# One scan for both directions in the S5 token mixer of a two-layer diffusion block

## The chip, the cores and the metric

The kernel runs on one core of a Trainium2 chip, in one launch that computes both layers. The metric is the device time of that launch in microseconds. Three runs of the kernel before gave 2297.36, 2298.63 and 2300.72 us, a median of 2298.63 us.

## The reference, cut to what matters

Two layers work on 256 context tokens and 512 latent tokens of width 1024. Each layer normalises the tokens, projects them and feeds four token mixers in parallel (A attention, B Fourier mixing, C a bidirectional diagonal state space "S5", D retention). Each mixer's output is projected to 1024 columns, gated, and added to a sum; an output projection and an MLP follow. The change is in mixer C alone:

```
lam_bar, b_bar = s5_discretise(...)             # per group of 16 channels: 64 complex states
bu = einsum('blgh,gph->blgp', u, b_bar)         # 16 groups
x[t] = lam_bar * x[t-1] + bu[t]                 # forward: context, then latent, carried over
                                                # backward: the context reversed, then the latent reversed
y = Re(C_f x_f) + Re(C_b x_b) + d * u           # readout and direct term
y = gelu(y);  val, gate = split(y @ w_glu);  out = val * sigmoid(gate)
```

## The kernel before, in words

All matrix products split both factors into a high and a low part (`split`, L289: ScalarE copies the high part at L293, VectorE subtracts at L294) and run three matmuls for each product (L239 through `gemm` and `mm3`). Weights come by DMA on SyncE into `raw` (two buffers) or `raws` (one), and become `whi`/`wlo` (three buffers) or `whis`/`wlos` (two).

The S5 stage (`s5`, from L1502) works in chunks of 8 tokens: 96 chunks hold the 768 tokens. A group pair g (eight of them, two groups of channels each) runs like this. `states(g)` loads the pair's operators (one DMA into `S`, two into `M`), multiplies the chunks by them on TensorE (the result lies in a PSUM tile `b` of which there are two), turns each chunk's sum by a precomputed rotation so that the decay becomes real, scans over the chunks, and turns back. The chunk axis has 128 columns: 96 chunks and a second copy of the 32 context chunks, because the backward direction starts with the context. Forward states lie in rows 0 to 63 and backward states in rows 64 to 127, so two scans run per real and imaginary part, L1568 forward on one half of the rows and L1570 backward on the other. The products of the turns run on VectorE, their sums and differences on GpSimd (`sx<-sx` and `sX<-sx` in the rows). `readout(g)` runs 12 matmuls (two passes for each of 6) into the same PSUM tile, adds the direct term `d * u` on VectorE (`Y`), and applies gelu on ScalarE, GpSimd and VectorE. The direct term is prepared ahead of the loop by four GpSimd multiplies of `sb`.

The loop calls `states(g + 1)` ahead of `readout(g)`, and between them `self.tick(2)`, which takes two steps of a background job: the merge of mixer A (`merge_steps`), whose steps alternate between a gate product (weights of 512 KB, 24 times 512 columns and in layer 0 also 24 times 256) and a branch product (6 times as much), with a VectorE multiply (`gate`) and a GpSimd add (`xy`) behind each branch product. Two of the 16 steps run ahead of the stage. After the loop the second feature transpose, the GLU products and the merge of mixer C follow; the first two gate products of that merge need nothing of the stage.

The order on each engine is set ahead by a planner: it simulates the program with modelled durations and gives each engine the most urgent ready instruction, where earlier in the program is more urgent. On the chip each engine then runs its list in order. A tile whose buffers are all in use holds the instruction that wants one.

The operators are prepared earlier (`s5_prep`): in layer 0 beside the merge of mixer B (about 104 to 205 us), in layer 1 beside the MLP of layer 0. `s5_rot` builds the rotations by doubling, the first 10 groups on VectorE and 6 on GpSimd; `s5_ops` builds the operators and the `strip`, from which `M` is read.

Of the kernel before, what the change touches and what calls it, by code (L numbers as in the profile page):

```python
# [9 lines left out]
F32 = mybir.dt.float32  # L10
# [3 lines left out]
AF = mybir.ActivationFunctionType  # L14
OP = mybir.AluOpType
# [8 lines left out]
NTOK = NCTX + NLAT  # L24
DEPTH = 2
# [184 lines left out]
class Net:  # L210
# [207 lines left out]
    def build(self):  # L418
        tc, nc = self.tc, self.nc
        with ExitStack() as es:  # L420
# [14 lines left out]
            self.xsp = self.dr.tile([KT, 128, NTOK], F32, name="xsp")  # L435
            self.scr = [self.dr.tile([8, 128, 6 * 256], F32, name=f"scr{l}") for l in range(DEPTH)]
            self.par = [self.dr.tile([128, 16 * NPAR + 48], F32, name=f"par{l}") for l in range(DEPTH)]
# [946 lines left out]
    def s5_ops(self, l, sp, bc, pr, pi, wr, wi, Br, Bi, Vr, Vi):  # L1384
        nc = self.nc
# [30 lines left out]
        def second(g, R, Wr, Wi):  # L1416
# [41 lines left out]
    def s5_rot(self, l, sp, rot):  # L1458

        nc = self.nc  # L1460
        F, B = slice(0, 64), slice(64, 128)
        T = lambda n, s, b=1: sp.tile([128] + list(s), F32, name=n, bufs=b)
        er, ei = T("er", [16, 128]), T("ei", [16, 128])
        nc.vector.memset(er[:, :, 0:1], 1.0)
        nc.vector.memset(ei[:, :, 0:1], 0.0)
        gr, gi = T("gr", [16, 1], 2), T("gi", [16, 1], 2)
        nc.vector.tensor_copy(gr[:, :, 0], rot[:, 0])
        self.ts(gi[F, :, 0], rot[F, 1], -1.0)
        nc.vector.tensor_copy(gi[B, :, 0], rot[B, 1])
        n = 1  # L1470
        while n < 128:
            m = min(n, 32)
            for o in range(0, n, m):
                t = [T(f"ce{k}", [16, 32], 1) for k in range(2)]
# [15 lines left out]
            if n > 4:  # L1490
                yield
        for k, e in enumerate((er, ei)):
            nc.vector.memset(e[F, :, 127:128], 0.0)
            nc.vector.memset(e[B, :, 0:1], 0.0)
        for _ in range(4):
            yield
        for k, e in enumerate((er, ei)):
            c = 1024 + 256 * k
            nc.sync.dma_start(self.scr[l][:, :, c:c + 256].rearrange("g p c -> p g c"), e.rearrange("p (g q) n -> p g (q n)", q=2))
        yield  # L1500

    def s5(self, l, sp, segs):  # L1502
# [22 lines left out]
        for g in range(16):  # L1525
# [8 lines left out]
        d4 = dv[:96].rearrange("c (g h) -> c g h", g=16)  # L1534
        for g in range(0, 16, 4):
            self.tt(Uc[:96, g:g + 4], Uc[:96, g:g + 4], d4[:, g:g + 4, None, :].to_broadcast([96, 4, 8, 16]), OP.mult, gp)
        G = T("sd", [8, 256])
        def states(g):

            S = T("S", [6, 2, 128], 2)  # L1540
            r8 = T("r8", [256], 2)
            self.act(r8.rearrange("p (q c) -> p q c", q=2), ex[:, 2 * g:2 * g + 2, None].to_broadcast([128, 2, 128]))
            nc.vector.memset(r8[F, 128:129], 0.0)
            nc.vector.memset(r8[B, 127:128], 0.0)
            nc.sync.dma_start(S, self.scr[l][g])
            M = T("M", [2, 128], 2)
            st = self.strip[l][2 * g:2 * g + 2]
            for q in range(2):
                nc.sync.dma_start(M[:, q], bass.AP(tensor=st.tensor, offset=st.offset + q * 3840,
                                                   ap=[[16, 8], [240, 16], [1, 128]]))  # L1550
            p = self.pb()
            for k in range(2):
                for q in range(2):
                    self.mm(p[:, 512 * k + 128 * q:512 * k + 128 * q + 128], S[:, k, q], U[:, 2 * g + q], True, True)
            w = p.rearrange("p (k c) -> p k c", k=2)[:, :, 0:256]
            f = lambda t: t.rearrange("p k q c -> p k (q c)")
            cs, sc = f(S[:, 4:6]), f(S[:, 5:3:-1])
            n = lambda: T("sx", [2, 256], 4)
            t1, t2, W = n(), n(), n()
            self.tt(t1, w, cs, OP.mult)  # L1560
            self.tt(t2, w, sc, OP.mult)
            self.tt(W[:, 0], t1[:, 0], t1[:, 1], OP.subtract, gp)
            self.tt(W[:, 1], t2[:, 0], t2[:, 1], OP.add, gp)
            Z = n()
            gp.memset(Z[F, :, 0:1], 0.0)
            gp.memset(Z[B, :, 255:256], 0.0)
            for k in range(2):
                nc.vector.tensor_tensor_scan(out=Z[F, k, 1:256], data0=r8[F, 1:256], data1=W[F, k, 0:255], initial=0.0,  # L1568
                                             op0=OP.mult, op1=OP.add)
                nc.vector.tensor_tensor_scan(out=Z[B, k, 254::-1], data0=r8[B, 254::-1], data1=W[B, k, 255:0:-1], initial=0.0,  # L1570
                                             op0=OP.mult, op1=OP.add)
            X = T("sX", [2, 256], 2)
            t1, t2 = n(), n()
            self.tt(t1, Z, cs, OP.mult)
            self.tt(t2, Z, sc, OP.mult)
            self.tt(X[:, 0], t1[:, 0], t1[:, 1], OP.add, gp)
            self.tt(X[:, 1], t2[:, 1], t2[:, 0], OP.subtract, gp)
            if segs[0][0] == 0:
                v = X[B].rearrange("p k (q c) -> p (k q) c", q=2)
                self.act(v[:, :, 0:32], v[:, :, 96:128])  # L1580
            return p, S, M, X

        def readout(g, p, S, M, X):
            for q in range(2):
                o = p[:96, 256 + 128 * q:384 + 128 * q]
                c = slice(128 * q, 128 * q + 96)
                self.mm(o, U[:, 2 * g + q, 0:96], M[:, q], True, False)
                self.mm(o, X[:, 0, c], S[:, 2, q], False, False)
                self.mm(o, X[:, 1, c], S[:, 3, q], False, True)
            Y = sp.tile([96, 2, 8, 16], F32, name="Y", bufs=2)  # L1590
            Z = sp.tile([96, 2, 8, 16], F32, name="Z", bufs=2)
            self.tt(Y, p[:96, 256:512].rearrange("c (q t h) -> c q t h", q=2, t=8), Uc[:96, 2 * g:2 * g + 2, ::-1, :], OP.add)
# [16 lines left out]

        r = states(0)  # L1610
        for g in range(8):
            n = states(g + 1) if g < 7 else None
            self.tick(2)
            readout(g, *r)
            r = n
            if g == 4:
                gT = [feature(0, *(self.fix.tile([128, NTOK], F32R, name="tmp", bufs=2) for _ in range(2)))]
# [5 lines left out]
        for m in range(2):  # L1623
            pv, pg = self.pb(), self.pb()
            self.gemm(pg, self.wk(w, 2, 256 + 128 * m, 384 + 128 * m), gT, segs)
            self.gemm(pv, self.wk(w, 2, 128 * m, 128 * m + 128), gT, segs)
            t = sp.tile([128, NTOK], F32, name="sd")
# [40 lines left out]
```

## Time and profile before

| of the profiled execution | |
|---|---|
| its time | 2295.92 us |
| its span in the trace | 2294.1 us |
| TensorE busy | 2172.5 us, 95% |
| VectorE, ScalarE, GpSimd busy | 1501.1, 727.3 and 329.3 us |
| mean granted TensorE clock | 0.981 |
| median of three runs | 2298.63 us |

The S5 stages lie at 538 to 674 us (layer 0) and 1733 to 1843 us (layer 1). In the rows, PE is TensorE, DVE VectorE, ACT ScalarE, POOL GpSimd and SPq the queue of SyncE. `b<-sa,S` are the chunk sums, `b<-M,sa` and `b<-S,sX` the readout, `b<-ident,sd` the feature transposes, `mm<-...` the background merge. "Idle before" is the time in which the engine had nothing running ahead of the instruction, with the instruction that ended it.

### The profile page before, as it was taken

The numbers are of one execution on the slowest core, as the hardware profiler recorded it, in microseconds if no ns is written. First come the engines' busy times: TensorE is split into PE (matmuls) and PEld (weight loads), VectorE is DVE, ScalarE is ACT, GpSimd is POOL, SyncE is SP. The second block draws the span as 40 slices with busy tenths as digits, with TensorE's granted clock in tenths as the row PEclk, the third lists the DMA queues.
The fourth block names the chain that finished last, engine by engine and source line by source line (L and its number), as shares of the span: only waits on it lengthen the run. The fifth ranks groups of instructions, "written<-read, shape, count | busy, mean of one in ns | idle before, by whom it ended". The sixth has DMA issues, their size and how long they took to land.

```text
span 2294.1 us, 32460 instructions
## 1 busy us (share of the span) xinstructions
PE 2172.5 (95%) x12438; PEld 1848.2 (81%) x12438; DVE 1501.1 (65%) x3283; ACT 727.3 (32%) x1226; POOL 329.3 (14%) x373
## 2 busy tenths in 40 slices
PE   7988999999989999999989999999998799999999
PEld 1867987888778888888878888987777678888887
DVE  5587889976753567777795447667746756554444
ACT  3412233443322341222212235234532234322322
POOL 2061110102421010000061101100014520000000
PEclk8998999999999999999999999999999899999999
DMA  8334233312312424535323232112132332333332
GB/s 261 111 110 131 84 97 127 115 63 90 110 52 78 133 80 152 187 129 180 113 85 106 85 111 70 60 56 77 51 110 91 97 121 86 101 93 100 93 101 92
DMA packets 112027, 240.26 MB, mean 105 GB/s; under 512 B 15744, under 2 KB 43264, under 8 KB 111872
## 3 DMA queue, kind: packets, MB, share of 16 engines
q1 hardware_dynamic: 111872, 238.19, 32.8%
q8 instruction: 98, 1.61, 0.3%
q14 instruction: 57, 0.47, 0.1%
HBM read 219.21 MB, written 18.93 MB: 104 GB/s over the span
## 4 chain that ended last, share of the span: by engine, by line
PE 68%; DVE 16%; issue 5%; DMA 4%; POOL 3%; ACT 3%; SPq 1%; POOLq 0%; ACTq 0%; DVEq 0%
PE mm L239 42%; PE b L239 24%; PE b L242 3%; DVE wlo L294 1%; DMA raw<-wst 1%; DVE olo L491 1%; DVE sx L1570 1%; POOL sX L245 1%; DVE xy L255 1%; DVE sx L1568 1%; DVE sx L245 1%; DVE S L245 1%; DMA adp<-wst 1%; ACT whi L293 1%; DMA par<-par 1%
## 5 line engine op out<-in xcount | busy, mean ns | idle before, releaser
L239 PE MATMUL mm<-hhi,wlo 128*128 128x256 f32 (+1 forms) x1768 | 537.3, 357 | 13.8 <-DVE wlo L294 10.0
L239 PE MATMUL mm<-hlo,whi 128*128 128x256 f32 (+1 forms) x1768 | 537.3, 357 | 3.3 <-POOL hlo L245 3.2
L239 PE MATMUL mm<-hhi,whi 128*128 128x256 f32 (+1 forms) x1768 | 535.8, 357 | 0.0
L294 DVE TENSOR_TENSOR wlo<-raw,whi 128x1024 fp32r<-128x1024 f32 (+2 forms) x238 | 297.8, 1252 | 161.3 <-ACT whi L293 160.9
L239 PEld LDWEIGHTS mm<-hhi,wlo 128*128 128x128 f32 x1768 | 333.9, 190 | 62.1 <-issue 11.4
L239 PEld LDWEIGHTS mm<-hlo,whi 128*128 128x128 f32 x1768 | 334.5, 190 | 51.4 <-POOL hlo L245 6.2
L239 PEld LDWEIGHTS mm<-hhi,whi 128*128 128x128 f32 x1768 | 335.1, 190 | 46.4
L293 ACT ACTIVATE whi<-raw 128x1024 fp32r<-128x1024 f32 (+2 forms) x238 | 246.5, 1037 | 376.9 <-PE b L239 303.8
L239 PE MATMUL b<-uh,wlo 128*128 128x256 f32 (+1 forms) x704 | 215.6, 360 | 10.6 <-DVE xy L255 5.8
L255 DVE SCALAR_TENSOR_TENSOR xy<-b,mod,xy 128x256 f32<-128x256 f32 (+1 forms) x192 | 121.8, 658 | 147.8 <-PE b L239 147.5
L239 PE MATMUL b<-ul,whi 128*128 128x256 f32 (+1 forms) x704 | 214.6, 358 | 0.1
L239 PE MATMUL b<-uh,whi 128*128 128x256 f32 (+1 forms) x704 | 214.5, 358 | 0.0
L239 PEld LDWEIGHTS b<-uh,wlo 128*128 128x128 f32 x704 | 132.3, 189 | 34.4 <-ACT uh L293 6.6
L245 DVE TENSOR_TENSOR tmp<-tmp 128x768 f32<-128x768 f32 (+1 forms) x64 | 53.1, 829 | 162.0 <-ACT tmp L258 161.9
L245 POOL TENSOR_TENSOR xy<-xy,gate 128x768 f32<-128x768 f32 (+1 forms) x48 | 85.0, 1773 | 485.4 <-DVE gate L255 389.1
L239 PEld LDWEIGHTS b<-ul,whi 128*128 128x128 f32 x704 | 132.9, 190 | 21.2 <-DVE ul L294 0.8
L239 PEld LDWEIGHTS b<-uh,whi 128*128 128x128 f32 x704 | 132.7, 189 | 19.4
L258 ACT ACTIVATE tmp<-mm 128x768 f32<-128x768 f32 (+3 forms) x86 | 51.5, 599 | 287.9 <-PE mm L239 267.9
L239 PE MATMUL mm<-whi,hlo 128*128 128x256 f32 (+1 forms) x424 | 124.3, 293 | 7.5 <-ACT rk L258 3.9
L239 PE MATMUL mm<-wlo,hhi 128*128 128x256 f32 (+1 forms) x424 | 124.3, 293 | 1.4 <-DVE wlo L294 1.4
L239 PE MATMUL mm<-whi,hhi 128*128 128x256 f32 (+1 forms) x424 | 123.0, 290 | 0.0
L258 ACT ACTIVATE gate<-mm 128x768 f32<-128x768 f32 (+1 forms) x64 | 44.9, 701 | 158.9 <-PE mm L239 158.7
(464 smaller groups left out, 3515.9 us busy)
## 6 DMA issues: line engine op xcount, KB each, us to landing
raw<-wst SPq DMA_DIRECT2D x236, 512.0 KB
adr<-wst SPq DMA_DIRECT2D x96, 256.0 KB
S<-scr SPq DMA_DIRECT2D x16, 768.0 KB
olo<-wst SPq DMA_DIRECT2D x42, 256.0 KB
adp<-wst SPq DMA_DIRECT2D x32, 256.0 KB
raws<-wst SPq DMA_DIRECT2D x64, 128.0 KB
xy<-xT SPq DMA_DIRECT2D x16, 384.0 KB
ohi<-wst SPq DMA_DIRECT2D x22, 256.0 KB
```

What stands on the lines that cost most here:

```text
L239: return self.nc.tensor.matmul(out, a, b, start=start, stop=stop)
L242: self.nc.tensor.transpose(out, a, self.ident[:n, :n])
L245: (eng or self.nc.vector).tensor_tensor(out=out, in0=a, in1=b, op=op)
L255: (eng or self.nc.vector).scalar_tensor_tensor(out, a, s, b, op0=op0, op1=op1)
L258: self.nc.scalar.activation(out, a, f, **kw)
L293: self.last_hi = self.nc.scalar.activation(hi, src, AF.Copy)
L294: return (eng or self.nc.vector).tensor_tensor(out=lo, in0=src, in1=hi.bitcast(F32), op=OP.subtract)
L491: self.nc.vector.tensor_tensor_reduce(out=junk, in0=r, in1=c[:, v], scale=1.0, scalar=0.0, op0=OP.mult, op1=OP.add, accum_out=acc[:, v:v + 1])
L1568: nc.vector.tensor_tensor_scan(out=Z[F, k, 1:256], data0=r8[F, 1:256], data1=W[F, k, 0:255], initial=0.0, op0=OP.mult, op1=OP.add)
L1570: nc.vector.tensor_tensor_scan(out=Z[B, k, 254::-1], data0=r8[B, 254::-1], data1=W[B, k, 255:0:-1], initial=0.0, op0=OP.mult, op1=OP.add)
```

## The change

The backward rows are reordered by ScalarE when it copies the sums out of PSUM, so that both directions run forward in one scan over 96 chunks; two extra columns hold zeros between the two groups of a pair. ScalarE puts the backward rows back in order afterwards. The sums and differences of the turns move from GpSimd to VectorE: a table with a third block, the negated sine, lets one subtraction serve both parts. The direct term goes into the strip when the operators are prepared. Two of the gelu's steps merge into one VectorE instruction, which reads PSUM. The loop becomes a pipeline of three steps: in step i the sums of pair i, the loads of pair i + 2, two background steps, the scan of pair i - 1 and the readout of pair i - 2. The operators of a pair come by five DMAs instead of three. One small `memset` stays on GpSimd; the `xy` adds of the merge stay there too.

```diff
+NCH = 96
+CW = NCH + 2
+NSCR = 1024 + 6 * CW
...
@@ s5_prep
+        dd = sp.tile([16, 16, 16], F32, name="dd")
+        a, b = PRM_OFF['d']
+        nc.sync.dma_start(dd.rearrange("p g h -> p (g h)"), self.prm[l][:16, a:b])
+        self.tt(dd, dd, self.ident[:16, None, :16].to_broadcast([16, 16, 16]), OP.mult)
...
@@ s5_ops
+            self.tt(k0, k0, dd[:, 2 * g:2 * g + 2], OP.add, nc.gpsimd)
             self.tt(ks[:, :, 7], ks[:, :, 7], k0, OP.add, nc.gpsimd)
@@ s5_rot
-        while n < 128:
+        while n < NCH:
             m = min(n, 32)
-            for o in range(0, n, m):
+            for o in range(0, min(n, NCH - n), m):
...
+        store(1, er)
+        store(2, ei)
+        self.act(ei, ei, scale=-1.0)
+        store(0, ei)
@@ s5
-        for g in range(0, 16, 4):
-            self.tt(Uc[:96, g:g + 4], Uc[:96, g:g + 4], d4[...].to_broadcast([96, 4, 8, 16]), OP.mult, gp)
-        G = T("sd", [8, 256])
-        def states(g):
...
+        G = T("sb", [8, 256])
+        ws = [T(f"w{k}", [2, 2, CW]) for k in range(2)]
+        Zs = [T(f"z{k}", [2, 2 * CW]) for k in range(2)]
...
+        def load(g):
+            src = self.scr[l][g]
+            A, B_, C, M = T("oA", [2, 2, 128], 2), T("oB", [3, 2 * CW], 2), T("oC", [2, 2, 128], 3), T("M", [2, 128], 3)
+            for t, a in ((A, 0), (B_, 1024), (C, 512)):
+                n = math.prod(t.shape[1:])
+                nc.sync.dma_start(t, src[:, a:a + n])
...
+            r8 = T("r8", [2, CW], 2)
+            self.act(r8, ex[:, 2 * g:2 * g + 2, None].to_broadcast([128, 2, CW]))
+            gp.memset(r8[:, 1, 0:1], 0.0)
+            return A, B_, C, M, r8.rearrange("p q c -> p (q c)")
+        def sums(g, A):
+            p = self.pb()
+            for k in range(2):
+                for q in range(2):
+                    self.mm(p[:, 512 * k + 128 * q:512 * k + 128 * q + 128], A[:, k, q], U[:, 2 * g + q], True, True)
+            v = ...
+            w = ws[g % 2]
+            self.act(w[F, :, :, 0:NCH], v[F, :, :, 0:NCH])
+            self.act(w[B, :, :, 0:NCH], v[B, :, :, 127:127 - NCH:-1])
+        def scan(g, B_, r8):
+            def turn(src):
+                t = T("sx", [2, 2, 2 * CW])
+                v = T("sv", [2, 2 * CW], 2)
+                self.tt(t[:, 0], src, B_[:, 1:3], OP.mult)
+                self.tt(t[:, 1], src, B_[:, 0:2], OP.mult)
+                self.tt(v, t[:, :, 0], t[:, :, 1], OP.subtract)
+                return v
+            W = turn(f(ws[g % 2]))
+            Z = Zs[g % 2]
             for k in range(2):
-                ...two scans, forward on rows F and backward on rows B
+                nc.vector.tensor_tensor_scan(out=Z[:, k, 1:], data0=r8[:, 1:], data1=W[:, k, 0:2 * CW - 1], initial=0.0,
                                              op0=OP.mult, op1=OP.add)
+            V = h(turn(Z))
+            X = T("sX", [2, 2, NCH], 2)
+            self.act(X[F], V[F, :, :, 0:NCH])
+            self.act(X[B, :, :, 0:32], V[B, :, :, 31::-1])
+            self.act(X[B, :, :, 32:], V[B, :, :, 95:31:-1])
+            return X
+        def readout(g, C, M, X):
+            p = self.pb()
...
-            self.tt(Y, p[...], Uc[:96, 2 * g:2 * g + 2, ::-1, :], OP.add)
+            Y = p[:96, :256].rearrange("c (q t h) -> c q t h", q=2, t=8)
             self.act(Z, Y, AF.Square)
-            self.act(Z, Z, scale=0.044715, bias=1.0)
-            self.tt(Z, Z, Y, OP.mult, gp)
-            self.act(Z, Z, AF.Tanh, scale=math.sqrt(2 / math.pi))
+            self.stt(Z, Z, 1 / 0.044715, Y, OP.add, OP.mult)
+            self.act(Z, Z, AF.Tanh, scale=0.044715 * math.sqrt(2 / math.pi))
...
+        ops = [load(0), load(1)]
+        X = {}
+        for i in range(10):
+            if i < 8:
+                sums(i, ops[i][0])
+            if i + 2 < 8:
+                ops.append(load(i + 2))
+            if i < 8:
+                self.tick(2)
+            if 0 < i < 9:
+                X[i - 1] = scan(i - 1, ops[i - 1][1], ops[i - 1][4])
+            if i > 1:
+                readout(i - 2, ops[i - 2][2], ops[i - 2][3], X.pop(i - 2))
+            if i == 6:
                 gT = [feature(0, ...)]
```

## Rows read from the trace of the kernel before

**Rows 1.** The page's first part, busy time and share of the span.
```profile
PE 2172.5 (95%) x12438; PEld 1848.2 (81%) x12438; DVE 1501.1 (65%) x3283; ACT 727.3 (32%) x1226; POOL 329.3 (14%) x373
```
**Rows 2.** Windows over the two S5 stages; columns as the header says.
```profile
core 0: us, PE busy (x) PEld busy (x) DVE busy (x) ACT busy (x) POOL busy (x), PEclk, DMA share, GB/s
543.70:667.10 123.40, 104.91 (x628) 91.72 (x628) 84.84 (x127) 34.30 (x65) 55.40 (x68) 0.93 0.28 92
1737.40:1838.50 101.10, 81.54 (x402) 66.57 (x400) 81.47 (x125) 29.82 (x56) 56.41 (x67) 0.90 0.32 104
```
**Rows 3.** TensorE's timeline: start, us, instruction, idle before and what ended it.
```profile
656.52 1.17 PE L239 MATMUL b<-S,sX 128*96 128x128 f32 x4 [4.90 <-ACT sX L258]
...
1765.26 1.16 PE L239 MATMUL b<-sa,S 128*128 128x128 f32 x8 [1.90 <-DVE Y L245]
...
1777.00 1.57 PE L239 MATMUL b<-sa,S 128*128 128x128 f32 x8 [2.39 <-DVE Y L245]
...
1782.12 0.38 PE L239 MATMUL b<-M,sa 128*96 128x128 f32 x2
...
1783.35 0.47 PE L239 MATMUL mm<-hhi,wlo 128*128 128x512 f32 x1
...
1787.54 0.39 PE L239 MATMUL mm<-hhi,wlo 128*128 128x512 f32 x1
```
**Rows 4.** VectorE's groups by shape, 1737.4 to 1838.5: count, busy, mean ns.
```profile
L245 DVE TENSOR_TENSOR sx<-sx,S 128x512 f32<-128x512 f32 x16 | 15.7, 1022 | 0.1
L1570 DVE TENSOR_TENSOR_SCAN sx<-r,sx 64x255 f32<-64x255 f32 x16 | 14.0, 875 | 0.2
L294 DVE TENSOR_TENSOR wlo<-raw,whi 128x1024 fp32r<-128x1024 f32 x7 | 11.2, 1602 | 0.5 <-ACT whi L293 0.5
L1568 DVE TENSOR_TENSOR_SCAN sx<-r,sx 64x255 f32<-64x255 f32 x16 | 10.9, 680 | 4.0 <-POOL sx L1565 3.9
L255 DVE SCALAR_TENSOR_TENSOR sd<-Z,Y 96x128 f32<-96x128 f32 x16 | 4.6, 320 | 7.2 <-ACT Z L258 7.1
L245 DVE TENSOR_TENSOR Y<-b,sb 96x256 f32<-96x256 f32 x8 | 3.3, 411 | 2.7 <-PE b L239 2.7
```
**Rows 5.** The same view, 543.7 to 667.1.
```profile
L294 DVE TENSOR_TENSOR wlos<-raws,whis 128x256 fp32r<-128x256 f32 x8 | 11.3, 1413 | 3.7 <-ACT whis L293 3.7
L294 DVE TENSOR_TENSOR wlo<-raw,whi 128x1024 fp32r<-128x1024 f32 x7 | 8.5, 1217 | 10.3 <-ACT whi L293 10.3
```
**Rows 6.** VectorE instructions on tile sx over the span, ns min/median/max.
```profile
L245 DVE TENSOR_TENSOR sx<-b,S x32: 671/680/692, 549.0 to 1820.9; 128x512 f32<-128x512 f32 x32
L245 DVE TENSOR_TENSOR sx<-sx,S x32: 678/687/1780, 554.7 to 1826.4; 128x512 f32<-128x512 f32 x32
```
**Rows 7.** VectorE's timeline: a row of 384 elements, and the short weight split undisturbed.
```profile
538.26 0.55 DVE L294 TENSOR_TENSOR olo<-K,ohi 128x384 fp32r<-128x384 f32 x1
...
1765.35 0.42 DVE L294 TENSOR_TENSOR wlos<-raws,whis 128x256 fp32r<-128x256 f32 x1
```
**Rows 8.** ScalarE's groups by shape, 543.7 to 667.1, and So's row from its tile view.
```profile
L258 ACT ACTIVATE Z<-Z 96x256 f32<-96x256 f32 x16 | 6.7, 417 | 8.8 <-POOL Z L245 8.6
L258 ACT ACTIVATE r<-ex 128x256 f32<-128x256 f32 x6 | 2.5, 416 | 31.6 <-DVE sx L1570 31.6
L258 ACT ACTIVATE sX<-sX 64x128 f32<-64x128 f32 x8 | 2.5, 307 | 21.2 <-POOL sX L245 21.2
...
L258 ACT ACTIVATE So<-b x16: 569/572/601, 137.8 to 1322.5; 128x512 f32<-128x512 f32 x16
```
**Rows 9.** GpSimd's adds of the merge by shape, 1737.4 to 1838.5.
```profile
L245 POOL TENSOR_TENSOR xy<-xy,gate 128x512 f32<-128x512 f32 x8 | 13.4, 1677 | 14.7 <-DVE gate L255 14.7
```
**Rows 10.** SyncE's own waits, 543.7 to 667.1: us in total, times, longest.
```profile
SPq L1549 <- PE b L239: 58.5, 6, 12.6
```
**Rows 11.** Layer 0's preparation: VectorE's rotation rows, and TensorE's wait behind them.
```profile
153.31 0.79 DVE L245 TENSOR_TENSOR ei<-ei,ce 128x320 f32<-128x320 f32 x1
...
159.18 0.59 PE L239 MATMUL mm<-hhi,wlo 128*128 128x256 f32 x2 [4.72 <-DVE wlo L294]
```

More of the change, by code (lines that the diff above doesn't have):

```diff
@@ L435, in build @@
             self.xsp = self.dr.tile([KT, 128, NTOK], F32, name="xsp")
-            self.scr = [self.dr.tile([8, 128, 6 * 256], F32, name=f"scr{l}") for l in range(DEPTH)]
+            self.scr = [self.dr.tile([8, 128, NSCR], F32, name=f"scr{l}") for l in range(DEPTH)]
             self.par = [self.dr.tile([128, 16 * NPAR + 48], F32, name=f"par{l}") for l in range(DEPTH)]
@@ L1491, in s5_rot, with store @@
                 yield
-        for k, e in enumerate((er, ei)):
-            nc.vector.memset(e[F, :, 127:128], 0.0)
-            nc.vector.memset(e[B, :, 0:1], 0.0)
         for _ in range(4):
             yield
-        for k, e in enumerate((er, ei)):
-            c = 1024 + 256 * k
-            nc.sync.dma_start(self.scr[l][:, :, c:c + 256].rearrange("g p c -> p g c"), e.rearrange("p (g q) n -> p g (q n)", q=2))
+        def store(k, e):
+            c = 1024 + 2 * CW * k
+            nc.sync.dma_start(self.scr[l][:, :, c:c + 2 * CW].rearrange("g p c -> p g c"), e.rearrange("p (g q) n -> p g (q n)", q=2))
+        store(1, er)
+        store(2, ei)
+        self.act(ei, ei, scale=-1.0)
+        store(0, ei)
         yield
@@ L1533, in s5 @@
                 self.act(U[:, g - 7:g + 1, 96:128], v[:, :, 0:32])
-        d4 = dv[:96].rearrange("c (g h) -> c g h", g=16)
-        for g in range(0, 16, 4):
-            self.tt(Uc[:96, g:g + 4], Uc[:96, g:g + 4], d4[:, g:g + 4, None, :].to_broadcast([96, 4, 8, 16]), OP.mult, gp)
-        G = T("sd", [8, 256])
-        def states(g):
[L1540 to L1546, printed above, removed]
+        G = T("sb", [8, 256])
+        ws = [T(f"w{k}", [2, 2, CW]) for k in range(2)]
+        Zs = [T(f"z{k}", [2, 2 * CW]) for k in range(2)]
+        for w, z in zip(ws, Zs):
+            nc.vector.memset(w[:, :, :, NCH:], 0.0)
+            nc.vector.memset(z[:, :, 0:1], 0.0)
+        f = lambda t: t.rearrange("p k q c -> p k (q c)")
+        h = lambda t: t.rearrange("p k (q c) -> p k q c", q=2)
+        def load(g):
[4 more added lines that the diff above has]
+                nc.sync.dma_start(t, src[:, a:a + n])
             st = self.strip[l][2 * g:2 * g + 2]
@@ L1553, in states @@
                 for q in range(2):
[L1554 to L1561, printed above, removed]
@@ L1569, in states @@
                                              op0=OP.mult, op1=OP.add)
[L1570 to L1583, printed above, removed]
+            V = h(turn(Z))
[6 more added lines that the diff above has]
+            p = self.pb()
@@ L1584, in readout @@
             for q in range(2):
-                o = p[:96, 256 + 128 * q:384 + 128 * q]
-                c = slice(128 * q, 128 * q + 96)
+                o = p[:96, 128 * q:128 * q + 128]
                 self.mm(o, U[:, 2 * g + q, 0:96], M[:, q], True, False)
-                self.mm(o, X[:, 0, c], S[:, 2, q], False, False)
-                self.mm(o, X[:, 1, c], S[:, 3, q], False, True)
-            Y = sp.tile([96, 2, 8, 16], F32, name="Y", bufs=2)
+                self.mm(o, X[:, 0, q], C[:, 0, q], False, False)
@@ L1608, in feature @@
             return hi, lo
[L1610 to L1616, printed above, removed]
+        ops = [load(0), load(1)]
[12 more added lines that the diff above has]
+            if i == 6:
                 gT = [feature(0, *(self.fix.tile([128, NTOK], F32R, name="tmp", bufs=2) for _ in range(2)))]
@@ L1626, in s5 @@
             self.gemm(pv, self.wk(w, 2, 128 * m, 128 * m + 128), gT, segs)
-            t = sp.tile([128, NTOK], F32, name="sd")
+            t = sp.tile([128, NTOK], F32, name="sb")
             self.act(t[:, a:b], pg[:, 256 + a:256 + b], AF.Tanh, scale=0.5)
```

25 lines of the change are left out of this document (9 added, 16 removed).

## The prediction

> **What bounds the kernel now.** I read the busy shares first: TensorE is busy 95% of the span [rows 1], so a change to mixer C can gain only where TensorE stands still or runs slowly. The windows over the two S5 stages come next. In layer 0 TensorE is busy 104.91 of 123.40 us, in layer 1 81.54 of 101.10: idle 18.5 and 19.6 us. The granted clock is 0.93 and 0.90, and VectorE is busy 81.47 of 101.10 us in layer 1 [rows 2]. The timeline says what ends the idle time: the sums of the next pair wait for the `Y` of the pair before, which frees their PSUM tile (1.90 and 2.39 us), and at the end the readout waits for the turned states (4.90 us) [rows 3]. After the 4.90 us gap four readout passes take 1.17 us, while all twelve of a later readout take 1.23 (1782.12 to 1783.35) [rows 3]: the clock is then at 1.2 instead of 2.4 GHz. So each pair's chain from VectorE to GpSimd and back is longer than what TensorE has beside it. A pair takes 11.74 us in layer 1 (1765.26 to 1777.00) [rows 3].
>
> How much is there to win? Idle time is 38.1 us. The lost clock costs at most (1 - 0.93) x 123.4 x 0.85 busy = 7.3 us in layer 0, and 0.10 x 101.1 x 0.81 = 8.2 us in layer 1 [rows 2]. So with TensorE never waiting the stages would take 97.6 and 73.3 us, 53.6 us less in all.
>
> **VectorE, pair by pair.** Removed in layer 1 per pair: two products from PSUM at 0.68, two from SBUF at 1.02 in the mean, four scans (10.9 + 14.0 us over 8 pairs: 3.11), `Y` 0.41 [rows 4, 6]; with two 0.06 memsets of r8 that is 7.0 us. The two `sd` (0.58) stay. Added: six operations of 392 elements. A row of 384 takes 0.55, one of 512 takes 0.68 [rows 6, 7]; I take 0.56, nearest the first, 3.36 in all. Two scans of 195 elements on all rows: between 195/255 x 0.68 = 0.52 and an unchanged 0.68 [rows 4]; I take 0.56. The gelu step on 256 elements: 0.41, like `Y`. Sum 4.9, so 2.1 us less a pair, 17 us a stage in layer 1; in layer 0, where the products from SBUF cost no more than the median 0.69, some 1.4 a pair, 11 us.
>
> GpSimd's work beside it matters as well: `wlos` takes 1.41 us in layer 0 and 0.42 undisturbed, `wlo` 1.60 in layer 1 and 1.22 in layer 0 [rows 4, 5, 7]. Those are the disturbed ones; without GpSimd's sums beside them 8 x 0.99 = 8 us go in layer 0 and 7 x 0.38 = 2.7 in layer 1. What stays is GpSimd's `xy`, 1.68 us each [rows 9].
>
> Products with one operand in PSUM never took over 0.692 us, those with both in SBUF up to 1.780 [rows 6]. After the change all six have both in SBUF. The Trainium skill (SBUF — State Buffer, section "Who interferes with whom") says the same as a rule: a VectorE instruction with two SBUF inputs contends with a GpSimd instruction that reads SBUF, one with a single SBUF input does not. That speaks against this change, which brings two formerly exempt products, and two subtractions that GpSimd did, under it. If each of 8 `xy` holds one operation by 1.780 - 0.678 = 1.1 us [rows 6], a stage pays 8.8 us; if none meets one, nothing. I keep both ends.
>
> VectorE's load is then 84.8 - 11 - 8 = 66 to 75 us in layer 0 against TensorE's 97.6, and 81.5 - 17 - 2.7 = 62 to 71 in layer 1 against 73.3. So TensorE becomes the bound, with ample room in layer 0 and little in layer 1.
>
> **ScalarE.** Removed: one gelu pass (0.42) and in layer 0 the copy of 64x128 (0.31). Added: two copies of 64x384, between 0.417 (256 elements) and 0.572 (512), so 0.50 each, and three copies of X, 0.50 + 0.31 + 0.42 [rows 8]. Net 1.5 to 1.8 us a pair, 12 to 14 a stage: ScalarE goes from 34 and 30 us busy [rows 2] to about 46 and 44. No row shows a reversed read on ScalarE; between the forward price and twice that it adds nothing to 1.2 us a pair. I take nothing, because the backward scans undisturbed cost what the forward ones cost (875 in the mean against 680 only beside GpSimd) [rows 4]. All of it lies beside TensorE except in the last pair.
>
> **TensorE and the loads.** The matmuls are the same ones. The readout has a PSUM tile of its own, and the sums' tile is free after two ScalarE copies instead of after `Y`, so the 1.90 and 2.39 us waits go; next late is the weight split on VectorE. Two more DMAs a pair cost SyncE some 0.45 us each; it stands waiting for buffers anyway, 58.5 us in layer 0 for `M` alone [rows 10]. `B_` and r8 have two buffers and wait for the scan of two pairs before. Behind them on SyncE stand weight loads; behind r8 on ScalarE, which already stood 31.6 us ahead of it [rows 8], stand copies. I take no cost, since a gate product is prefetched; the other end is the last rival.
>
> **Ends of the stage.** The background job has 14 steps left, two per iteration: it is used up at i = 6, while scans run on. From the last sums on: copies 1.0, scan with both turns 8 x 0.56 = 4.5, X 1.2, readout 1.23 (1782.12 to 1783.35 [rows 3]), gelu 0.42 + 0.41 + 0.42 + 0.58, transposes 0.9: 10.7 us. Beside it TensorE has two earlier readouts (2.5) and the first gate product of the next merge: 19 rows from 1783.35 to 1787.54 make 24 take 5.6 us in layer 1 [rows 3], about 8.5 with layer 0's extra columns. That leaves 2.6 us idle in layer 1 (8.2 without the gate) and 0 to 8 in layer 0; I take 5 and 4, and 2 each for the low clock after it.
>
> **Stalls that stay.** One list per engine means some will: half a microsecond a pair, 4 us in layer 1, 3 in layer 0 (bounds 0 and the 19 us of today).
>
> **Sum for the stages.** Layer 0: 97.6 + 4 + 2 + 3 = 106.6, gain 16.8. Layer 1: 73.3 + 5 + 2 + 4 = 84.3, gain 16.8.
>
> **Preparation.** The rotation loses its last block: 6 VectorE operations of 0.79 us (12 rows of the kind end at 153.31) and 6 on GpSimd; 4.7 us of VectorE ahead of a weight split for which TensorE waits 4.72 us in layer 0 [rows 11]. Added are one small product, one ScalarE negation, a third store and 8 tiny GpSimd adds, all beside that. Between 0 and 5 us gained there; I take 3. In layer 1 the same work lies beside the MLP: nothing.
>
> Together 16.8 + 16.8 + 3 = 36.6 us. The profiled execution took 2295.92 us, its span 2294.1; the median of the runs is 2.7 us above it. 2295.9 - 36.6 = 2259.3 on the profile's scale, 2298.6 - 36.6 = **2262 us** on the median's.
>
> **Rivals.**
>
> *VectorE still ends the loop.* In layer 1 its 71 us with contention is nearly TensorE's 73.3, and in-order waits for ScalarE's copies lie on top. For: 81% busy today [rows 2]. Against: only the upper end comes near. Layer 1 then gains 6, layer 0 10, preparation 2: 2281 us. The rule named above is this rival's mechanism.
>
> *Everything fits.* No stall, no drain, 5 us from the preparation: 2298.6 - 53.6 - 5 = 2240 us. Against: the drain is longer than its cover.
>
> *The gain is given back.* The change does what it says, but the next merge's two gate products, used as fill, are missing behind the GLU, and the drain after i = 6 is as long as today's gaps: within 4 us of 2298.
>
> *ScalarE ties the pairs together, slower.* ScalarE now stands at both ends of the scan. If r8 of pair i + 2, urgent because early in the program, is put ahead of the next copies, they wait for the scan of pair i; likewise `B_` ahead of the weights on SyncE. Serial, a pair costs sums 0.9, copies 1.0, scan 4.5, X 1.2, readout 1.2, gelu 1.8, plus background weight copies on ScalarE and VectorE of 2 to 4: 13 to 15 us. It decides from 11.7 us a pair in layer 1 on. At 13.5 there and layer 0 unchanged: 8 x 1.76 - 3 = +11, so 2310 us. For: the 31.6 us already waited [rows 8]. Against: the scan is two steps ahead of its readout.
>
> **Chances.** Forecast 0.55 (its own range 2249 to 2274), VectorE 0.22, all fits 0.08, given back 0.06, ScalarE 0.09. The range 2244 to 2291 leaves out the slower case, most of the unchanged one and part of the best: about 2 in 10. No change means within 0.2%, about what a measurement of this kernel can tell, so 2294.0 to 2303.2: faster 0.85, same 0.06, slower 0.09.
>
> **What would show it.** Right: stages of about 107 and 84 us, clock over 0.95 in both, no wait of the sums for `Y`; VectorE under 75 us in each; six operations near 0.56 and two scans near 0.56 a pair; the wait near 159 us gone. Wrong: pairs of over 11 us in layer 1, sums waiting for ScalarE's copies, weight splits late behind `B_`, or over 10 us idle ahead of the second feature transpose.

## The result, and the profile after

The changed kernel takes 2246.18 us (median of 4 runs, 2245.12 to 2251.3) against 2299.68 for the kernel before in the same session: ratio 0.9775, 95% interval 0.9761 to 0.9788. The forecast was 2262.0 with a range of 2244 to 2291. The range holds the time, the forecast's own range (2249 to 2274) doesn't. The direction and the mechanism were right, and the gain is larger than forecast: 53.5 us between these medians, where 36.6 were forecast. The traces account for 49.0 us, the difference of the spans of the two profiled executions (2294.1 and 2245.1 us); the profiled execution of the kernel before took 2295.92 us, less than each of its four runs, and no trace shows the rest.

The windows of [rows 2] in the changed kernel, between the same events. Layer 0's begins with the last transposes `b<-ident,sa` ahead of the sums, layer 1's with the first sums; both end where the GLU's first `b<-sa,whi` begins:
```profile
core 0: us, PE busy (x) PEld busy (x) DVE busy (x) ACT busy (x) POOL busy (x), PEclk, DMA share, GB/s
532.50:640.70 108.20, 102.60 (x647) 91.77 (x647) 75.50 (x116) 46.28 (x91) 16.58 (x14) 0.97 0.38 110
1709.30:1788.30 79.00, 74.20 (x409) 63.24 (x406) 65.54 (x113) 42.38 (x88) 12.43 (x14) 0.98 0.44 132
```
123.40 us became 108.20 and 101.10 became 79.00. TensorE's idle time fell from 18.5 and 19.6 us to 5.6 and 4.8, the granted clock rose from 0.93 and 0.90 to 0.97 and 0.98, and GpSimd went from about 56 us in each to 17 and 12. In layer 0 TensorE also does more background work inside the window, 19 matmuls of the merges or some 3.4 us (439 `mm` matmuls take 79.60 us there; before there were 420). That work no longer has to be done behind the window, so this comparison understates layer 0's gain by as much.

TensorE's timeline, to be held against [rows 3] (start, us, instruction, idle before and what ended it):
```profile
621.72 2.08 PE L242 MATMUL b<-sa,oA 128*128 128x128 f32 x8 [4.75 <-DVE tmp L258]
...
635.74 0.85 PE L245 MATMUL b<-ident,sb 96*128 96x96 f32 x8
...
1749.19 1.06 PE L242 MATMUL b<-sa,oA 128*128 128x128 f32 x8
...
1758.23 1.06 PE L242 MATMUL b<-sa,oA 128*128 128x128 f32 x8
...
1762.94 0.46 PE L242 MATMUL b<-M,sa 128*96 128x128 f32 x2 [0.91 <-ACT w L261]
...
1770.18 1.64 PE L242 MATMUL b<-sa,oA 128*128 128x128 f32 x8 [2.92 <-DVE tmp L258]
...
1786.66 0.50 PE L242 MATMUL b<-sa,wlo 128*128 128x512 f32 x1 [0.75 <-ACT sa L261]
```
A pair in layer 1 takes 9.04 us (1749.19 to 1758.23) instead of 11.74, and its sums wait for nothing. One wait of size is left in each layer, 4.75 and 2.92 us: the last sums need the PSUM tile of the first feature transposes, which VectorE reads late. From the last sums on, 14.0 us in each layer (621.72 to 635.74, 1770.18 to 1784.14), TensorE has no gap before the second transposes.

VectorE's groups by shape over layer 0's loop (count, busy us, mean ns, idle before), against [rows 4, 5]:
```profile
L297 DVE TENSOR_TENSOR wlo<-raw,whi 128x1024 fp32r<-128x1024 f32 x6 | 11.7, 1947 | 10.2 <-ACT whi L296 10.0
L248 DVE TENSOR_TENSOR sx<-z,oB 128x392 f32<-128x392 f32 x16 | 10.0, 664 | 0.2
L297 DVE TENSOR_TENSOR wlos<-raws,whis 128x256 fp32r<-128x256 f32 x8 | 9.8, 1227 | 0.1
L248 DVE TENSOR_TENSOR sv<-sx 128x392 f32<-128x392 f32 x16 | 9.0, 564 | 0.6
L248 DVE TENSOR_TENSOR sx<-w,oB 128x392 f32<-128x392 f32 x16 | 8.3, 556 | 5.8 <-ACT w L261 5.8
L1593 DVE TENSOR_TENSOR_SCAN z<-r,sv 128x195 f32<-128x195 f32 x16 | 8.1, 550 | 0.6
L258 DVE SCALAR_TENSOR_TENSOR gate<-gate,mm 128x768 f32<-128x768 f32 x8 | 7.6, 945 | 7.8 <-PE mm L242 7.8
```
The new operations cost what was forecast (0.56 us) in all but one of their instructions: each kind has a mean of 0.55 to 0.57 us but `sx<-z`, where one product of 2.17 us, begun inside one of GpSimd's additions, lifts it to 0.66. The two weight splits don't: 1947 and 1227 ns. These means mix two cases, which VectorE and GpSimd show side by side:
```profile
568.88 0.42 DVE L297 TENSOR_TENSOR wlos<-raws,whis 128x256 fp32r<-128x256 f32 x1
...
569.04 1.95 POOL L248 TENSOR_TENSOR xy<-xy,gate 128x768 f32<-128x768 f32 x1 [4.88 <-DVE gate L258]
...
569.45 2.62 DVE L297 TENSOR_TENSOR wlo<-raw,whi 128x1024 fp32r<-128x1024 f32 x1 [0.16 <-ACT whi L296]
```
The first split began ahead of the addition and kept its 0.42 us, the second began inside it and took 2.62. Of the 14 splits of layer 0's loop seven began inside an addition (short ones 1.90 to 2.09 us, long ones 2.62 to 2.69); the seven others took 0.41 to 0.42 and 1.23 us.

In the preparation the wait of [rows 11] is gone and its neighbours stay:
```profile
142.90 0.98 PE L242 MATMUL mm<-hhi,wlo 128*128 128x256 f32 x2 [3.20 <-DVE wlo L297]
...
185.12 0.98 PE L242 MATMUL mm<-ohi,wlos 128*128 128x256 f32 x2 [3.58 <-DVE wlos L297]
```

**Where the 49.0 us came from.** For all kernels below one measure is used that doesn't depend on how the loop puts work off: from the first sums of a stage to the last product of the merge behind it. Before it is 201.9 us (layer 0, from 547.91) and 151.5 (layer 1, from 1737.45), after 183.6 (from 536.66) and 128.8 (from 1709.32). The spans differ by 11.2 up to layer 0's first sums, 18.3 in its stage, -1.4 between, 22.6 in layer 1's stage, -1.7 behind: 49.0.

### The profile page after: what moved, and what is told of

The parts are those of the page before. It is cut to its first block, busy times and chain, and to the rows that moved or that the text cites. A ratio compares the mean times of both kernels' runs of the same rounds, so it can differ in the third digit from the quotient of the medians.

```text
span 2245.1 us, 32471 instructions
## 1 busy us (share of the span) xinstructions
PE 2156.7 (96%) x12438; PEld 1838.9 (82%) x12438; DVE 1466.9 (65%) x3243; ACT 753.1 (34%) x1284; POOL 252.5 (11%) x273
## 4 chain that ended last, share of the span: by engine, by line
PE 74%; DVE 13%; DMA 5%; issue 4%; ACT 2%; POOL 1%; SPq 0%; ACTq 0%; POOLq 0%; DVEq 0%
PE mm L242 47%; PE b L242 25%; PE b L245 3%; DMA raw<-wst 2%; DVE wlo L297 1%; DVE olo L494 1%; DVE xy L258 1%; DMA adp<-wst 1%; DVE S L248 1%; DMA par<-par 1%; ACT whi L296 1%; DMA crow<-csil 1%; POOL hlo L248 0%; DVE R L248 0%; DVE gate L258 0%
## 5 line engine op out<-in xcount | busy, mean ns | idle before, releaser
L248 POOL TENSOR_TENSOR xy<-xy,gate 128x768 f32<-128x768 f32 (+1 forms) x48 | 84.3, 1758 | 529.6 <-DVE gate L258 493.9
```

Of the source, the lines that this page charges most:

```text
L248: (eng or self.nc.vector).tensor_tensor(out=out, in0=a, in1=b, op=op)
```

## The experiments

The kernel before took 2303 to 2304 us in the sessions of the experiments, so they are compared by their ratio to it (the changed kernel: 0.9775) and by their stages, each from one profiled execution. What an edit did to a stage is read from the stage: elsewhere the spans of the variants differ by up to 5 us (e11's first sums come 4.9 us later than e8's, and 4.5 us of it are made up ahead of layer 1).

| kernel | ratio (95%) | stage, layer 0 | stage, layer 1 |
|---|---|---|---|
| before | 1 | 201.9 | 151.5 |
| changed | 0.9775 (0.9761-0.9788) | 183.6 | 128.8 |
| e1 table's last quarter back | 0.9800 (0.9775-0.9824) | 183.1 | 130.0 |
| e2 before, without it | 0.9973 (0.9959-0.9988) | 200.7 | 151.5 |
| e3 first transposes later | 0.9785 (0.9764-0.9806) | 184.5 | 129.2 |
| e4 no fill | 0.9868 (0.9839-0.9896) | 194.4 | 140.7 |
| e5 two steps | 0.9780 (0.9765-0.9795) | 185.7 | 130.5 |
| e6 four scans | 0.9793 (0.9777-0.9809) | 183.7 | 138.2 |
| e7 subtractions on GpSimd | 0.9799 (0.9785-0.9814) | 183.7 | 136.7 |
| e8 xy on VectorE | 0.9734 (0.9714-0.9753) | 178.0 | 126.2 |
| e9 e5, e6 and e7 together | 0.9927 (0.9912-0.9943) | 198.3 | 149.2 |
| e10 e8 and e5 | 0.9741 (0.9725-0.9758) | 180.9 | 127.2 |
| e11 xy of all merges on VectorE | 0.9717 (0.9702-0.9731) | 178.1 | 124.9 |
| e12 e6 and e7 | 0.9847 (0.9828-0.9866) | 187.7 | 143.2 |

**e1 and e2: the preparation's part.** In the changed kernel, with the block written to a scratch tile `xr`:
```
-            for o in range(0, min(n, NCH - n), m):
+            for o in range(0, n, m):
+                spare = n + o >= NCH
...
```


> The changed kernel, with the fourth quarter of the rotations' table computed again (columns 96 to 127, ten more of the 320-column operations on VectorE and GpSimd at the place where the kernel before had them), into scratch that nobody reads. It undoes the preparation's part alone. Theory (the part is worth 9 to 11 us, because the 4.72 us wait behind it also opened the waits after it and held the granted clock down): 2255 to 2258 us against 2246.2, the weight split near 153 us late by 4 to 5 us again, the clock of the 12 us after it back to about 0.90. Rival (the forecast's term: only the wait itself): 2249 us, and everything behind 159 us merely shifted.

In the kernel before:
```
-            for o in range(0, n, m):
+            for o in range(0, min(n, 96 - n), m):
```
Two memsets, not shown, set the columns that are left out to zero.


> The kernel before, without the last quarter of the rotations' table (columns 96 to 127 are zero instead: the S5 branch leaves out what depends on them). It does the preparation's part alone. Theory: 9 to 11 us off, 2289 to 2291 us, the wait of 4.72 us at 159.18 gone and the stage's start near 250 instead of 260.7. Rival (the forecast's term of 3 us): 2296 to 2297 us. The two S5 stages stay at 123 and 101 us in both.

The mark is the first transpose of `dcy`, the end of the preparation's busy part: 260.7 us before, 250.1 after. In e1 it comes at 257.8, in the ten other variants of the changed kernel between 250.9 and 253.1 (mean 252.2): 5.6 us for the block. In e2 it comes at 256.8: 3.9 us. Both lie between the two theories, and so do the times (0.25% or 5.8 us more than the changed kernel, 0.27% or 6.2 us less than the one before). The times by themselves are weak: e1's interval overlaps that of the changed kernel, and e2's allows a gain of 2.8 to 9.4 us. TensorE's waits of over 1 us between 140 and 200 us, first e1, then e2, then the two of the kernel before beside the one in [rows 11]:
```profile
144.62 0.59 PE L242 MATMUL mm<-hhi,wlo 128*128 128x256 f32 x2 [4.72 <-DVE wlo L297]
...
160.60 0.98 PE L242 MATMUL mm<-hhi,wlo 128*128 128x256 f32 x2 [3.77 <-DVE wlo L297]
...
193.28 0.98 PE L242 MATMUL mm<-ohi,wlos 128*128 128x256 f32 x2 [3.86 <-DVE wlos L297]
```
```profile
143.42 0.98 PE L239 MATMUL mm<-hhi,wlo 128*128 128x256 f32 x2 [3.19 <-DVE wlo L294]
...
189.41 0.98 PE L239 MATMUL mm<-ohi,wlos 128*128 128x256 f32 x2 [7.08 <-DVE wlos L294]
```
```profile
142.25 0.68 PE L239 MATMUL mm<-hhi,wlo 128*128 128x256 f32 x2 [4.70 <-DVE wlo L294]
...
191.49 0.98 PE L239 MATMUL mm<-ohi,wlos 128*128 128x256 f32 x2 [4.21 <-DVE wlos L294]
```
With the block back, the wait near 160 us is there again (3.77 us), and the 12 us from 160.60 on run at a granted clock of 0.79; in the changed kernel 155.40 to 167.40 has 1.00. So e1 pays the wait and up to 2.5 us of clock, which together cover its 5.6 us; the rival counted the wait alone. Without the block in the kernel before, that wait goes, but the one near 190 grows from 4.21 us to 7.08: part of what one wait gave was taken by the next.

The kernel before and the changed one differ at another place ahead of the mark. From the end of TensorE's wait for `rk` (3.9 us before, 2.7 in e2, 1.3 in the changed kernel, 0.6 in e1) to the mark, in the order before, e2, changed, e1:
```profile
215.37:260.72 45.35, 44.43 (x350) 44.05 (x350) 36.76 (x121) 13.41 (x31) 7.73 (x12) 0.94 0.30 88
...
211.39:256.79 45.40, 43.60 (x349) 43.02 (x350) 37.83 (x121) 13.44 (x31) 8.11 (x12) 0.96 0.29 85
...
207.28:250.12 42.84, 41.93 (x349) 41.55 (x350) 37.21 (x122) 13.73 (x32) 7.75 (x12) 1.00 0.30 93
...
215.00:257.84 42.84, 41.93 (x350) 41.55 (x350) 37.30 (x122) 13.70 (x32) 7.75 (x12) 1.00 0.31 93
```
The same work takes 2.5 us less where the granted clock is 1.00, behind the two shorter waits.

**e3: first transposes one turn later.**
```
-            if i == 6:
+            if i == 7:
                 gT = [feature(0, ...)]
```


> The changed kernel, with the first feature transpose one turn of the loop later (behind the last sums instead of ahead of them). In the profile of the changed kernel the last sums wait 4.75 us (layer 0) and 2.92 us (layer 1) for that transpose's PSUM tile, whose reader stands in VectorE's queue. Theory (the wait is lost time that the order makes): 5 to 8 us off, 2238 to 2241 us, the two gaps under 1 us. Rival (VectorE's queue sets this end in any case, and the readout or the second transpose waits instead): 2245 to 2247 us.

The rival holds. The last sums no longer wait, and the readout waits in their place:
```profile
622.30 0.74 PE L242 MATMUL b<-M,sa 128*96 128x128 f32 x2 [4.25 <-ACT w L261]
...
1775.91 0.46 PE L242 MATMUL b<-M,sa 128*96 128x128 f32 x2 [2.00 <-ACT w L261]
```
There are two PSUM tiles of this kind; the place in the list only chooses who waits for the one held.

**e4: no fill.**
```
+                with ExitStack() as es:
+                    if n == 2 and m < 2:
+                        es.enter_context(self.tc.issue_after(self.last_mm.ins))
                     self.gemm(ps, self.wk(w, KT), self.h, segs)
```


> The changed kernel, with the first two gate products of the next merge held back until the GLU's last product. It takes away what TensorE does between the last sums and the second feature transpose. Theory (the end of each stage is free because these products fill it; without them TensorE stands idle for what is left of the drain of 10.7 us beside two readouts of 2.5): 5 to 8 us idle in each layer, 10 to 16 us in all, 2256 to 2262 us. Rival (the last pair's chain is short enough to end beside the readouts): under 3 us, 2246 to 2249 us.

The theory's mechanism holds, at more than its price: the stages grow by 10.8 and 11.9 us (5 to 8 expected). Layer 0's waits of over 1 us from the last sums on:
```profile
624.50 2.08 PE L242 MATMUL b<-sa,oA 128*128 128x128 f32 x8 [7.29 <-DVE tmp L258]
...
634.95 0.70 PE L242 MATMUL b<-oC,sX 128*96 128x128 f32 x4 [3.57 <-ACT sX L261]
...
638.96 1.51 PE L245 MATMUL b<-ident,sb 96*128 96x96 f32 x8 [2.03 <-DVE sb L258]
```
The drain itself is 14.5 us (624.50 to 638.96), 13.5 in layer 1. In layer 1 the clock from the second transposes to 23 us later is 0.77 (1.00 in the changed kernel).

**e5: two steps.** The loop of the kernel before, in the changed kernel:
```
...
+        sums(0, ops[0][0])
+        X = scan(0, ops[0][1], ops[0][4])
+        for g in range(8):
+            if g < 7:
+                sums(g + 1, ops[g + 1][0])
+                n = scan(g + 1, ops[g + 1][1], ops[g + 1][4])
...
+            self.tick(2)
+            readout(g, ops[g][2], ops[g][3], X)
```


> The changed kernel with the loop of the kernel before: scan g+1 right behind its sums, readout g in the same turn. Everything else (one scan, no GpSimd, 96 chunks) stays. From the first sums to the second feature transpose the changed kernel takes 99.1 us (layer 0) and 74.8 us (layer 1). Theory (VectorE then waits in each turn for sums and two copies, about 3 us a pair, with 70.1 and 63.9 us of work of its own: about 94 us a layer): layer 0 grows little, to 99 to 103, layer 1 becomes VectorE's, 88 to 96 us, 13 to 25 us in all. Rival (the two steps are enough, since VectorE's load fell and the queue holds other work to take): both stages within 2 us, no more than 4 us in all.

The rival holds: 2.1 and 1.6 us longer, the ratio unchanged within its interval. Up to the second transposes, the measure of its expectation, e5 is even shorter: 97.0 and 74.6 us against 99.1 and 74.8. The third step by itself is nearly worthless here.

**e6: four scans.**
```
+                for R in (F, B):
+                    nc.vector.tensor_tensor_scan(out=Z[R, k, 1:], data0=r8[R, 1:], ...)
```


> The changed kernel with four scans of 64 rows in a pair instead of two of 128 (one for each direction, as before). 16 scans of 195 columns more on VectorE, 0.55 us each: 8.8 us a layer. Theory (TensorE ends the loop, VectorE has 29 us to spare in layer 0 and 11 in layer 1): both stages within 1.5 us of 99.1 and 74.8, no more than 3 us in all; the one scan for both directions is not what the gain comes from, in layer 0 at least. Rival (VectorE still sets layer 1's period): layer 1 grows by 5 to 9 us.

Each theory has one layer: layer 0 grows by 0.1 us, layer 1 by 9.3, a little over the rival's 5 to 9. The windows from the first sums to the GLU:
```profile
539.32:639.18 99.86, 94.22 (x597) 84.00 (x595) 78.56 (x127) 41.83 (x87) 16.25 (x14) 0.98 0.36 103
1713.48:1799.90 86.42, 76.59 (x404) 64.58 (x402) 73.90 (x128) 40.44 (x87) 12.43 (x14) 0.94 0.41 121
```
VectorE at 78.56 of 99.86 costs nothing. In layer 1 the stage grows by about as much as VectorE's added work (the scans take 17.8 us instead of 8.8), though VectorE is idle for 12.5 of 86.42 us. In the changed kernel it was idle for 11.5 of the same window's 75.43 us, so its idle time did not take up the added work; that the order of its list holds it idle is likely and not shown.

**e7: the turns' subtractions on GpSimd.**
```
-                self.tt(v, t[:, :, 0], t[:, :, 1], OP.subtract)
+                self.tt(v, t[:, :, 0], t[:, :, 1], OP.subtract, gp)
```


> The changed kernel with the two subtractions of each pair's turns on GpSimd (a part of 'no GpSimd' undone: 16 operations of 392 columns a layer moved). Theory (in the three steps a longer chain is hidden; VectorE loses 8.8 us a layer and waits some 1 to 1.5 us for each, ahead of the scan and of the gelu steps): 0 to 4 us in layer 0, 2 to 8 us in layer 1. Rival (GpSimd's work slows VectorE's own beside it, as with the weight splits that took 1767 ns beside the xy additions and 1227 without): VectorE's products of the turns rise from 0.55 to over 0.8 us and both stages grow by 6 us or more.

The theory holds: 0.0 and 7.9 us. On GpSimd a subtraction takes 1040 ns in layer 1 instead of 564, and VectorE's scans there wait 8.1 us for them; the products beside stay at 0.56 to 0.59 us, so the rival falls. In layer 0 the scans wait 7.9 us as well, and it costs nothing.

**e8: the xy additions on VectorE.**
```
-  self.tt(self.y[m][:, a:b], ..., OP.add, self.nc.gpsimd)
+  self.tt(self.y[m][:, a:b], ..., OP.add, None if n == 0 else self.nc.gpsimd)
```


> The changed kernel with the eight xy additions of the merge that runs beside the S5 stage on VectorE instead of GpSimd. It takes away the last large GpSimd work in the stage (about 2.0 us each) and with it what it costs VectorE; it adds 8 operations of 512 to 768 columns (0.8 to 1.1 us) to VectorE. Theory (TensorE ends both stages): within 1.5 us of 99.1 and 74.8. Rival (the contention still costs the stage something, as the forecast had it with up to 8.8 us): 3 to 6 us off in layer 1, the weight splits back from 1767 to about 1230 ns in both cases.

The rival's mechanism holds, and in both layers: 5.6 and 2.7 us off (it had 3 to 6 in layer 1), and the long splits are back at 1221 ns. VectorE's groups over layer 0's loop, against those of the changed kernel above:
```profile
L258 DVE SCALAR_TENSOR_TENSOR gate<-gate,mm 128x768 f32<-128x768 f32 x8 | 7.6, 950 | 9.2 <-PE mm L242 9.2
L248 DVE TENSOR_TENSOR xy<-xy,gate 128x768 f32<-128x768 f32 x8 | 7.6, 948 | 0.0
L297 DVE TENSOR_TENSOR wlo<-raw,whi 128x1024 fp32r<-128x1024 f32 x6 | 7.3, 1221 | 11.7 <-ACT whi L296 11.7
...
L297 DVE TENSOR_TENSOR wlos<-raws,whis 128x256 fp32r<-128x256 f32 x8 | 3.3, 413 | 0.0
```
and the two windows from the first sums to the GLU:
```profile
538.10:632.95 94.85, 93.34 (x602) 83.39 (x600) 64.83 (x119) 42.17 (x87) 0.60 (x6) 1.00 0.37 109
1704.75:1777.64 72.89, 71.21 (x403) 60.66 (x402) 61.42 (x120) 40.52 (x87) 0.60 (x6) 1.00 0.48 143
```
VectorE does eight operations more and is busy for less: 64.83 us instead of 70.09. One addition costs it 0.95 us of its own. On GpSimd it took 2.0 us and cost VectorE (6 x 0.73 + 8 x 0.81 + 16 x 0.10) / 8 = 1.56 us in the operations beside it.

**e9 and e12: parts undone together.** e9 is e5, e6 and e7 in one, e12 only e6 and e7.

> The changed kernel with three parts undone together, each of which alone left layer 0's stage as it was or made it shorter (first sums to the GLU's first product: 97.6 us with two steps, 99.9 with four scans, 97.7 with the turns' subtractions on GpSimd, against 99.7): two steps, four scans of 64 rows, and the subtractions on GpSimd. Left of the change: 96 chunks instead of 128 columns, the direct term in the strip, ScalarE's copies. Theory (the parts stand in for each other: layer 0 has slack for any one, and the chain of a pair needs all three): layer 0 back to 108 to 116 us, layer 1 to 95 to 105 us (before: 115.6 and 97.3). Rival (what left the loop for good, GpSimd's products and the shorter rows, carries layer 0's gain): layer 0 no more than 102 us, layer 1 near 90.

> The kernel with three parts undone, but with its three steps back: four scans of 64 rows and the turns' subtractions on GpSimd alone. Measured from the first sums to the last product of the next merge, which holds work that the loop puts off: before 201.9 and 151.5 us, changed kernel 183.6 and 128.8, three parts undone 198.3 and 149.2. Theory (three steps hide a long chain wherever an engine has room; layer 0 has it, in layer 1 VectorE has none left for eight more scans and its waits for GpSimd): layer 0 at 183 to 187 us, so that the three steps are worth 11 us or more there although they were worth 2 in the changed kernel; layer 1 at 142 to 149. Rival (it is VectorE's load and its waits for GpSimd, not the order): layer 0 at 193 us or more.

In e9 14.7 of the 18.3 us of layer 0 are lost again and 20.3 of 22.6 in layer 1, though the parts alone cost 2.1, 0.1 and 0.0 us (sum 2.2) and 1.6, 9.3 and 7.9 (sum 18.8). In layer 1, where VectorE has little to spare, the parts nearly add up; in layer 0 each is hidden by the others. What e9 leaves, 3.6 and 2.3 us, is the rest of the change (96 columns instead of 128, the direct term in the strip, the readout's own PSUM tile, the gelu step); no run takes it apart. Up to the GLU's first product, the measure of its expectation, e9 takes 108.8 and 93.7 us (the theory had 108 to 116 and 95 to 105, the rival at most 102 and near 90: layer 0 decides, layer 1 lies between). e9's waits of over 3 us in layer 1 show a long chain again, in each of its places:
```profile
1764.13 0.79 PE L242 MATMUL mm<-hhi,wlo 128*128 128x512 f32 x1 [3.58 <-ACT gate L261]
...
1793.79 1.83 PE L242 MATMUL b<-sa,oA 128*128 128x128 f32 x8 [3.20 <-DVE tmp L258]
...
1818.21 1.17 PE L242 MATMUL b<-oC,sX 128*96 128x128 f32 x4 [5.38 <-ACT sX L261]
```
e12 puts the third step back: layer 0 at 187.7 us (0.7 over the theory's range, far from the rival's 193), layer 1 at 143.2. So the step that was worth 2.1 and 1.6 us is worth 10.6 and 6.0 when the chain is long.

**e10 and e11: towards a faster kernel.**

> The kernel with the xy additions on VectorE, and the loop of two steps as well. Theory (with VectorE relieved the order of the loop matters even less; two steps ended layer 0's stage 2.8 us sooner, as the sums no longer wait for the transposes' PSUM tile behind the readout): 0 to 3 us under the kernel with the additions alone, ratio to the kernel before 0.972 to 0.9735. Rival (two steps' own waits, 7.7 us in layer 0, are now the larger): 1 to 4 us above it, ratio 0.974 to 0.975.

> The xy additions of all the merges on VectorE, not only of the one beside the S5 stage (the two other merges of each layer too: 16 additions more a layer). Theory (the contention costs time only where VectorE has little to spare; the other merges are bound by TensorE): within 2 us of the kernel with the one merge's alone, ratio 0.9725 to 0.9745. Rival (GpSimd's additions slow the weight splits there as well and TensorE waits for those): 3 to 8 us less, ratio 0.970 to 0.972.

e10: its interval covers both theories; the stages, 2.9 and 1.0 us longer than e8's, speak for the rival. e11: its span is 1.1 us below e8's, as the theory has it, its ratio 0.9717 lies in the rival's range (0.970 to 0.972), and the intervals overlap: whether the other merges pay anything isn't settled. Both e8 (2240.32 us) and e11 (2238.16 us) are faster than the changed kernel and the one before.

## Why the prediction was right, and where its sizes failed

**The bound.** Right. With VectorE and GpSimd out of the pair's chain TensorE ends the loop in layer 0, by a margin (e6, e7: nothing). In layer 1 it does so narrowly, as the forecast said: some 9 us more on VectorE cost 9.3.

**VectorE's prices.** Right by themselves: 0.56 us (forecast 0.56) for the six operations, 0.55 (0.56) for a scan, 0.41 for the gelu step. VectorE is busy for 75.5 and 65.5 us, in layer 0 at the upper end of 66 to 75, in layer 1 inside 62 to 71. The cost of GpSimd's additions was bounded at 0 to 8.8 us a stage and measures, by e8, 12.5 and, with layer 1's groups, 7 x 0.47 + 8 x 0.44 + 16 x 0.03 = 7.3. It is past the upper end in layer 0: the bound took its price from the turns, and the weight splits pay most. The relief that the forecast credited to them, 8 and 2.7 us without GpSimd's sums, didn't come either: the short ones of layer 0 go from 1413 to 1227 ns, the long ones of layer 1 from 1602 to 1691, since the additions that stayed fall on them. The Trainium skill (SBUF — State Buffer, section "Who interferes with whom") has VectorE instructions with two SBUF inputs contend with a GpSimd instruction that reads SBUF, and spares those with one. By that rule, the traces agree: the splits lose, and the gate step, whose second input is in PSUM, doesn't. In the kernel before three gate steps that began while GpSimd ran `sX<-sx` (562.82, 575.15 and 588.82 us) took 953 ns each; in layer 0 of the changed kernel none ran beside GpSimd, and they take 945.

**ScalarE and the loads.** Right: 46.3 and 42.4 us busy (about 46 and 44); the copies take 0.48, and 0.52, 0.31 and 0.40 for X, read forward or reversed. No TensorE wait of the loop is for a load.

**The ends of the stage.** This term of the stages' sum failed. It set the drain against "two earlier readouts (2.5) and the first gate product of the next merge" and charged 4 and 5 us idle with 2 more each for the clock. Its own working gave 2.6 us idle in layer 1; it took 5 without giving a reason. Found: none in either layer up to the second transposes, and 0.8 and 1.0 us behind them. The drain is not shorter than forecast: 14.0 us from the last sums to the transposes in both layers (e4: 14.5 and 13.5), where the forecast's steps ahead of them make 9.8. The cover is longer: in layer 1 32 product rows stand there instead of the 24 counted, 7.5 us by [rows 3]'s 5.6 for 24, so the merge's second gate product is in it too. Nine more of its 48 rows stand ahead of the last sums (from 1764.94 us). e4 prices the two gate products' place at 10.8 and 11.9 us.

**The stalls that stay.** 3 and 4 us forecast, 4.8 and 3.8 found. They are not half a microsecond a pair but, all but 0.9 us in layer 1, one wait for a PSUM tile, which e3 could move and not remove. In e8 the same wait is 1.2 and 1.1 us.

**The stages' sum.** 108.2 us against 106.6, and 79.0 against 84.3. In layer 1 that is the 7 us for the ends, less the 1.0 found and the 0.9 by which TensorE's busy time exceeds its floor (74.2 against 73.3). In layer 0 the close match is partly luck: the 6 us for the ends, 0.8 found, are made up by a stall 1.8 us larger and by a busy time 5.0 us above the floor (102.6 against 97.6), 3.4 of it the merge's matmuls that came into the window and that the sum didn't count.

**The preparation.** The largest miss, and outside its own bounds: 3 us forecast (0 to 5), 10.6 between the two profiles. The forecast counted a wait and no clock behind it. The removed block accounts for 4 to 6 by e1 and e2. Some 2 us are the changed kernel's profile itself, which has the earliest mark of all. Of the other 3, 2.5 lie behind the wait for `rk`, where the granted clock is 1.00 instead of 0.94. The changed kernel keeps 1.00 there with the block back too (e1), and the kernel before has only 0.96 without it (e2), so it isn't the block; what shortened the wait ahead of it stays open.

**The rivals.** "Everything fits" (2240 us) came closest, since there was no drain to pay. "VectorE still ends the loop" is what e6 makes of layer 1. The given-back gain is e4: it takes 22 us, not all. Pairs tied together by ScalarE didn't happen: layer 1's pair is 9.04 us.

## What to carry to other kernels

When several edits shorten one chain and an engine has slack, each alone can look worthless, because the others hide it: undo them together before calling one useless. Before a drain is charged, count everything that the list holds behind the last step, not only the next product. An operation on GpSimd beside VectorE's two-input work is not free even if nobody waits for it: add what it takes from VectorE, and compare that with doing it there.

## What the runs showed of the hardware

A 128x768 addition took 2.0 us on GpSimd and 0.95 on VectorE. VectorE's splits of 128x1024 that began while it ran on GpSimd took 2.62 to 2.69 us instead of 1.22, and those of 128x256 1.90 to 2.09 instead of 0.41; a split that had begun ahead of the addition kept its 0.42. Moving the addition to the busier engine lowered that engine's busy time. A reversed read of 384 elements costs ScalarE the same 0.48 us as a forward one.
